# A decoder block on one core: squares read from the copied row, attention's low weight parts made by GpSimd, and the first gates' loads issued by GpSimd

## The chip, the core and the metric

The kernel runs on one core of a Trainium2 chip. The time is the device time of one execution in microseconds. The core has a matrix engine (PE), a vector engine (VectorE, DVE), an activation engine (ScalarE, ACT), GpSimd (POOL) and SyncE (SP), which issues most of the transfers. Each engine works through a queue of its own in order; between the queues, semaphores hold an instruction back until what it needs is done.

## What is computed

One layer over x of 1024 tokens by 1024 channels, in float32. Cut to what matters here:

```python
h = rms_norm(x, attn_norm_w)
q, k, v, u, g = split(h @ w_in)            # 1024 x 7168
q = rms_norm(q per head half); k = rms_norm(k per head half)
p = softmax(q1 k1^T * scale + bias, causal) - lam * softmax(q2 k2^T * scale + bias, causal)
y_a = (rms_norm(p @ v per head) * (1 - lam_init)) @ w_proj_attn
c = silu(layer_norm(causal_depthwise_conv(u_a * sigmoid(u_b), width 31)))
y_b = c @ w_proj_conv
x = x + (sigmoid(g_a) * y_a + sigmoid(g_b) * y_b) @ w_out
h = rms_norm(x); x = x + (silu(h @ W_gate) * (h @ W_up)) @ w_down
```

There are 8 heads; q and k are split into two halves of 64, v is 128 wide.

## The kernel before

Every product of float32 numbers is made of three matrix products: each operand is split in a high part, which ACT makes by a cast (`split_hi`, L120), and a low part, the original less the high part (`split_lo` on DVE, L125). L168, L169 and L170 are the three products. The weights pass through this split too: `wraw` is loaded, `whi` cast, `wlo` subtracted. Which engine subtracts a weight's low part is decided by a switch, `low_by_pool`: while it is set, `low` uses POOL (L131), otherwise DVE.

The stages follow one another in time roughly so:

- 0 to 248 us: normalized x, then the columns of V and u and the first conv tiles, with the switch set.
- 248 to 300 us: Q item 0 and the last of V.
- 300 to 822 us: attention. PE does heads 0 to 7 (scores `sc`, transposes `pT` of the weights, products `pW` with v), and fills the gaps with Q items 1 to 7 (`q_item`: a head's q and k columns, one `whi`/`wlo` pair for each half) and G items 0 to 15 (`g_item`: gate columns, one pair each, stored to `g_d`). On DVE the taps of the depthwise convolution (L594) run in between, one multiply-add for each of 31 taps, the first by ACT. The accumulator `acc` of a conv tile lies in PSUM for tiles 0 to 3 and in SBUF for tiles 4 to 7 (`CONV_PSUM` is 4).
- 822 to about 1000 us: the output projection of the heads (`aT`), gates for it, and the conv branch's layer norm and projection.
- After that w_out and the channel mixer, to 1726 us.

In attention L1291 adds the bias table `tb` to the scores in PSUM and takes the running maximum (E), L1296 on ACT exponentiates, L1306 forms the difference of the two softmax halves in `E` (SBUF), L1328 transposes it on PE.

A Q item works on banks `pg` of 512 columns in PSUM. For each bank ACT copies the bank to an SBUF row `raw` (tile name `qkraw`, L797) and makes eight squares of 64 columns with a running sum (L800, tile name `jk`), both from the bank; DVE then scales the row by the root (L807) and PE transposes it (L815). The rows are then split, and parts of them are copied between partitions by SP's transfers (L826 to L837), since two halves of 64 share 128 partitions. The first scores of the next head wait for those copies.

Heads 0 to 4 of the attention output are read back early from memory: five loads `early` (L1492) into attention's buffers `E`, of which there are four, each followed by a cast to `aTh` (ACT) and a low part `aTl` (DVE). Then follow `part`, a memset on POOL, the loads of heads 5 and 6, and `ln_step`, which begins the layer norm's chain for the mean: on SP a load of the conv tiles' sum and eight loads of `cT_lo`, then PE's `mean`. After it the first four gates are loaded by SP (`gated`, L1632) from `g_d`, and ACT takes their sigmoid (L1633); DVE multiplies them into the projection's banks (L1640).

The order of each engine's queue is not written out by hand: a scheduler lays the instructions out by the costs that it holds for them and by what depends on what, so that a moved piece of work moves others. What the program does fix are the conditions `after(...)`, by which a piece isn't issued before another.

Of the kernel before, what the change touches and what calls it, by code (L numbers as in the profile page):

```python
# [10 lines left out]
F32 = mybir.dt.float32  # L11
F32R = mybir.dt.float32r
AF = mybir.ActivationFunctionType
# [3 lines left out]
P = 128  # L17
# [3 lines left out]
HD = 64  # L21
VD = 128
# [35 lines left out]
def kernel(  # L58
# [27 lines left out]
    nc = tc.nc  # L86
    dve, act, pool, pe = nc.vector, nc.scalar, nc.gpsimd, nc.tensor
# [11 lines left out]
    sm = ctx.enter_context(tc.tile_pool(name="sm", bufs=4))  # L99
# [12 lines left out]
    def nm(s):  # L112
        uid[0] += 1
        return f"{s}_{uid[0]}"

    def f32(ap):
        return ap.bitcast(F32)
# [9 lines left out]
    low_by_pool = [False]  # L127
# [7 lines left out]
    def after(ins):  # L135

        return nullcontext() if ins is None else tc.issue_after(ins)

    def last_of(engine):
        for ins in reversed(nc.cur_bb.bb.instructions):  # L140
            if ins.engine == engine:
                return ins
# [11 lines left out]
    def pg():  # L154
        npg[0] += 1
        p_, tag = pgs[npg[0] % len(pgs)]
        return p_.tile([P, 512], F32, tag=tag, name=nm("pg"))
# [4 lines left out]
    def pm(z="pm"):  # L162
        npm[0] += 1
        p_, tag = pms[npm[0] % len(pms)]
        return p_.tile([P, 512], F32, tag=tag, name=nm(z))
# [86 lines left out]
    def pcol(key, k=0):  # L252
        c = col[key] + k
        return pvec[:, c : c + 1]
# [89 lines left out]
    class Stream:  # L344
# [12 lines left out]
        def next(self):  # L357
            self.fetch()
            return self.have.pop(0)
# [6 lines left out]
    def gemm_T(w, mhi, mlo, sb, amid=None):  # L366

        o = pg()
        cs = slice(sb * 512, (sb + 1) * 512)
        for k in range(NKT):  # L370
            mm3(o[:], w[0][:, k, :], w[1][:, k, :], kt(mhi, k)[:, cs], kt(mlo, k)[:, cs], k == 0, k == NKT - 1)
            if amid is not None and k == NKT // 2 - 1:
                amid()
        return o

    def gemm_N(o, halves, shi, slo, i):

        ts = slice(i * P, (i + 1) * P)
        for k in range(NKT):
            whi, wlo = halves[k // 4]  # L380
            mm3(o, kt(shi, k)[:, ts], kt(slo, k)[:, ts], whi[:, k % 4, :], wlo[:, k % 4, :], k == 0, k == NKT - 1)
# [8 lines left out]
    g_d = [dr.tile([P, S], F32, name=f"g_d{c}") for c in range(2 * NKT)]  # L390
# [289 lines left out]
    def rstd_of(ss, n, scale, fast=False):  # L680
        v = sm.tile([P, 16], F32, tag="v", name=nm("v"))[:, :n]
        dve.tensor_scalar(v, ss, scale, EPS, op0=ALU.mult, op1=ALU.add)
        return rsq(v, n, fast)
# [99 lines left out]
    T = {}  # L783
    late = []

    def q_item(h):
        halves = [ws.next(), ws.next()]
        t = {}
        T[h] = t
        for b in (1, 0):  # L790
            raw = qkp.tile([P, 4, 256], F32, tag="qkraw", name=nm("qkraw"), bufs=2)
            ss = sm.tile([P, 16], F32, tag="ss16", name=nm("ss16"))
            for i2 in range(2):
                o = pg()
                for e in range(2):
                    gemm_N(o[:, 256 * e : 256 * (e + 1)], halves, hT_hi, hT_lo, 4 * b + 2 * i2 + e)
                act.copy(raw[:, 2 * i2 : 2 * i2 + 2, :], o[:].rearrange("p (e c) -> p e c", c=256))  # L797
                jk = sm.tile([P, VD], F32, tag="jk", name=nm("jk"), bufs=1)[:, :HD]
                for g in range(8):
                    act.activation(  # L800
                        jk, o[:, g * HD : (g + 1) * HD], AF.Square, accum_out=ss[:, 8 * i2 + g : 8 * i2 + g + 1]
                    )
                if i2 == 0:
                    yield
            r = rstd_of(ss[:], 16, 1.0 / HD, fast=h > 0)
            r4 = raw[:].rearrange("p i (g d) -> p (i g) d", d=HD)
            dve.tensor_tensor(r4, r4, r.unsqueeze(2).to_broadcast([P, 16, HD]), op=ALU.mult)  # L807

            def turn_qk(z, key, b, raw):


                dma = nc.sync.dma_start
                pt = pm("pQ")
                for i in range(4):
                    pe.transpose(pt[:, i * P : (i + 1) * P], raw[:, i, z * P : (z + 1) * P], ident[:])  # L815
                w = pcol(key + "n")

                def part(j):
                    return qkp.tile([P, 512], F32R, tag=f"{key}s{j}", name=f"{key}s{j}_{h}_{b}", bufs=2 if key == "q" else 3)

                s1, s2 = part(1), part(2)
                act.activation(s1[:], pt[:], AF.Identity, scale=w)
                lo = part(3) if key == "q" else qkp.tile([P, 512], F32R, tag="klo", name=f"klo_{h}_{b}", bufs=1)
                dve.scalar_tensor_tensor(lo[:], pt[:], w, f32(s1[:]), op0=ALU.mult, op1=ALU.subtract)
                if key == "q":
                    dma(f32(s2[HD:, :]), f32(s1[HD:, :]))  # L826
                    lo2 = part(4)
                    for one, two in ((s1, s2), (lo, lo2)):
                        if one is lo:
                            dma(f32(two[HD:, :]), f32(one[HD:, :]))  # L830
                        dma(f32(two[:HD, :]), f32(one[HD:, :]))
                        dma(f32(one[HD:, :]), f32(one[:HD, :]))
                    t["q", b] = (s1, lo), (s2, lo2)
                else:
                    act.activation(s2[HD:, :], pt[HD:, :], AF.Identity, scale=w[HD:, :])
                    dma(f32(s2[:HD, :]), f32(lo[HD:, :]))
                    dma(f32(s1[HD:, :]), f32(lo[:HD, :]))  # L837
                    t["k", b] = s1, s2

            for z, key in ((1, "k"), (0, "q")):
                free = NT * (h - 1) + (0 if key == "k" and b else NT if key == "q" and not b else NT // 2)
                late.append((free if h else 0, lambda a_=(z, key, b, raw): turn_qk(*a_)))
            yield

    inatt = [False]
    MAKE = {"V": v_item, "U": u_item, "Q": q_item, "G": g_item}

    def run(items):  # L850
# [394 lines left out]
        due -= int(due)  # L1245
    while late:
        late.pop(0)[1]()
    low_by_pool[0] = False
    pcv_ctx.close()
    pgs.pop()  # L1250
    pg2_ctx.close()
# [264 lines left out]
    with after(m):  # L1516
        for _ in fill:
            pass
    inatt[0] = False
    del pms[1:]  # L1520
    at_ctx.close()

# [9 lines left out]
    for h in (5, 6):  # L1532
        for sb in range(2):
            cs = slice(sb * 512, (sb + 1) * 512)
# [79 lines left out]
    def ln_step():  # L1614
        for _ in range(lnp.pop(0)):
            next(lnq, None)
# [8 lines left out]
    lp = ln_ctx.enter_context(tc.tile_pool(name="lnp", bufs=2, reuse_waits="tile"))  # L1625
    gts, ngt = [(bp, "gt")], [0]

    def gated(d, cs):
        ngt[0] += 1
        p_, tag = gts[ngt[0] % len(gts)]  # L1630
        g = p_.tile([P, 512], F32, tag=tag, name=nm("gt"), bufs=4)
        nc.sync.dma_start(g[:], d[:, cs])  # L1632
        act.activation(g[:], g[:], AF.Sigmoid)  # L1633
        return g

    def ya_out(c, os2, gs=None):
        for sb in range(2):
            cs = slice(sb * 512, (sb + 1) * 512)
            g = gs[sb] if gs else gated(g_d[c], cs)
            dve.tensor_tensor(g[:], os2[sb][:], g[:], op=ALU.mult)  # L1640
            nc.sync.dma_start(ya_d[c][:, cs], g[:])

    ln_step()
    mean_hi = last_of(mybir.EngineType.Activation)

    NE = 2
    with after(last_of(mybir.EngineType.Activation)):
        g3 = [[gated(g_d[c], slice(sb * 512, (sb + 1) * 512)) for sb in range(2)] for c in range(NE)]
    first_gates = last_of(mybir.EngineType.Activation)
    w3 = [ws.next()]  # L1650
    with after(mean_hi), after(first_gates):
        w3.append(ws.next())
    o3 = [[pg() for sb in range(2)] for c in range(NE)]
    for k in range(NKT):
        for c in range(NE):
            for sb in range(2):
                cs = slice(sb * 512, (sb + 1) * 512)
                with after(last_mean[0]):
                    mm3(o3[c][sb][:], w3[c][0][:, k, :], w3[c][1][:, k, :], aT_hi[k][:, cs], aT_lo[k][:, cs], k == 0, k == NKT - 1)
        if k == NKT - 2:  # L1660
            with after(last_mm[0]):
                ln_step()
    for c in range(NE):
        ya_out(c, o3[c], g3[c])
    with after(first_gates):
        ln_step()
    for c in range(NE, NKT):
        with after(mean_hi if c == NE else None), after(first_gates if c == NE else None):
            w = ws.next()
# [11 lines left out]
    for cl in ((0, 1, 2), (3, 4), (5, 6), (7,)):  # L1681
        pair = [(c, ws.next()) for c in cl]
        for sb in range(2):
            cs = slice(sb * 512, (sb + 1) * 512)
            for c, w in pair:
                g = gated(g_d[NKT + c], cs)
                ya = bp.tile([P, 512], F32, tag="ya", name=nm("ya"), bufs=4)
                nc.sync.dma_start(ya[:], ya_d[c][:, cs])
                o = gemm_T(w, cT_hi, cT_lo, sb)
# [102 lines left out]
    o = {}  # L1792
# [342 lines left out]
```

## Time and profile before

| | us |
|---|---|
| median of 3 runs (lowest to highest) | 1726.91 (1726.63 to 1727.03) |
| span of the profiled execution | 1725.7 |
| median less span | 1.2 |
| PE busy | 1714.6 |
| DVE busy | 1275.4 |
| ACT busy | 862.5 |
| POOL busy | 219.1 |

The span runs from the first instruction to the last of one execution. The median of the runs is 1.2 us longer than it. Busy time counts the work of each engine and not its waits. A row of a group of instructions gives the line, the engine, the operation, output<-inputs with the shapes, how often it occurred, busy time and mean duration in ns, and the idle time of the engine just before, with what ended it. The views of a tile give minimum, median and maximum in ns, and the start of the first and of the last.

### The profile page before, as it was taken

Reading aid. Unit: us, or ns where it says so; the run is one execution under the profiler, and the core shown is the slowest. Engines: PE = TensorE matmul, PEld = TensorE weight load, DVE = VectorE, ACT = ScalarE, POOL = GpSimd, SP = SyncE. Lnnn points to the kernel's source line nnn. Section 1 sums busy time; section 2 is a strip of 40 time slices with the busy share of each in tenths; the row PEclk is TensorE's granted clock in tenths of the full one; section 3 lists DMA queues with packets and bytes.
Section 4 is the critical chain, followed back from the end, with each engine's and each line's share of the span. In section 5 each row is a group of like instructions: output and inputs, shape, how many; then the busy total and the mean of one; then the engine's idle time right before and its main releaser. Section 6 shows DMA issues by size and latency. Waiting matters only on the chain.

```text
span 1725.7 us, 25863 instructions
## 1 busy us (share of the span) xinstructions
PE 1714.6 (99%) x9243; PEld 1477.9 (86%) x9243; DVE 1275.4 (74%) x2128; ACT 862.5 (50%) x1958; POOL 219.1 (13%) x207
## 2 busy tenths in 40 slices
PE   9999999999999999999999999999999999999999
PEld 7997889998998998988788888888888888888887
DVE  7675889898988888878687769966676666575544
ACT  5333335767777776756556325633333333333332
POOL 3997851000000000000000000000000000000000
PEclk9999999999999999999999999999999999999999
DMA  6344445336345344343973683245455445598663
GB/s 208 116 126 132 131 151 154 104 109 171 104 127 147 115 125 138 101 136 130 333 238 118 200 296 119 74 135 164 147 170 170 154 141 164 175 355 285 217 215 130
DMA packets 261604, 281.64 MB, mean 163 GB/s; under 512 B 16546, under 2 KB 181986, under 8 KB 261475
## 3 DMA queue, kind: packets, MB, share of 16 engines
q1 hardware_dynamic: 254160, 267.71, 48.3%
q0 software_dynamic: 5680, 9.39, 2.6%
q10 hardware_dynamic: 1634, 2.89, 0.5%
q8 instruction: 73, 1.20, 0.3%
q14 instruction: 57, 0.46, 0.1%
HBM read 181.84 MB, written 85.50 MB: 155 GB/s over the span
## 4 chain that ended last, share of the span: by engine, by line
PE 92%; DMA 3%; DVE 2%; ACT 1%; issue 1%; POOL 0%; SPq 0%; DVEq 0%; POOLq 0%; ACTq 0%
PE acc L980 29%; PE acc L488 12%; PE pg L168 12%; PE pg L169 12%; PE pg L170 12%; PE wo L1850 3%; PE sc L1290 2%; PE sc L1289 2%; PE pT L1328 2%; PE pg L1106 1%; DVE acc L594 1%; PE pW L168 1%; PE pW L169 1%; PE pW L170 1%; PE pQ L815 1%
## 5 line engine op out<-in xcount | busy, mean ns | idle before, releaser
L594 DVE SCALAR_TENSOR_TENSOR acc<-u,cw,acc 128x1023 f32<-128x1023 f32 (+14 forms) x240 | 303.4, 1264 | 23.2 <-ACT acc L588 20.7
L170 PE MATMUL pg<-whi,hT_lo 128*128 128x256 f32 x704 | 200.2, 285 | 0.0
L168 PE MATMUL pg<-whi,hT_hi 128*128 128x256 f32 x704 | 199.7, 285 | 0.4 <-DVE v L125 0.4
L169 PE MATMUL pg<-wlo,hT_hi 128*128 128x256 f32 x704 | 199.5, 284 | 0.0
L125 DVE TENSOR_TENSOR wlo<-draw,whi 128x1024 fp32r<-128x1024 f32 x75 | 91.7, 1223 | 83.4 <-ACT whi L120 78.9
L120 ACT CAST whi<-draw 128x1024 fp32r<-128x1024 f32 x75 | 79.1, 1055 | 129.5 <-PE acc L488 114.3
L169 PEld LDWEIGHTS pg<-wlo,hT_hi 128*128 128x128 f32 x704 | 134.4, 191 | 1.8
L170 PEld LDWEIGHTS pg<-whi,hT_lo 128*128 128x128 f32 x704 | 134.3, 191 | 1.8
L168 PEld LDWEIGHTS pg<-whi,hT_hi 128*128 128x128 f32 x704 | 134.0, 191 | 2.1 <-DVE v L125 0.6
L120 ACT CAST whi<-wraw 128x1024 fp32r<-128x1024 f32 x90 | 94.7, 1052 | 70.6 <-PE pg L169 32.6
L488 PE MATMUL acc<-wlo,whi 128*128 128x512 f32 x308 | 119.8, 389 | 0.0
L488 PE MATMUL acc<-whi,wlo 128*128 128x512 f32 x308 | 119.8, 389 | 0.0
L1296 ACT ACTIVATE E<-E,mn 128x640 f32<-128x640 f32 (+7 forms) x128 | 99.8, 781 | 30.8 <-DVE mn L1291 29.2
L168 PE MATMUL pg<-hT_hi,whi 128*128 128x512 f32 x288 | 114.4, 397 | 0.1
L169 PE MATMUL pg<-hT_lo,whi 128*128 128x512 f32 x288 | 113.7, 395 | 0.0
L170 PE MATMUL pg<-hT_hi,wlo 128*128 128x512 f32 x288 | 113.7, 395 | 0.0
L120 ACT CAST whi<-s 128x1024 fp32r<-128x1024 f32 x54 | 56.9, 1053 | 104.9 <-PE acc L980 101.8
L125 DVE TENSOR_TENSOR wlo<-wraw,whi 128x1024 fp32r<-128x1024 f32 x75 | 93.3, 1246 | 12.6 <-ACT whi L120 12.3
L1291 DVE CUSTOM_DVE_ANT_0 E<-sc,tb 128x512 f32<-128x512 f32 (+3 forms) x128 | 74.2, 585 | 33.2 <-PE pT L1328 16.1
L980 PE MATMUL acc<-h_hi,whi 128*128 128x512 f32 x240 | 93.4, 389 | 0.0
L980 PE MATMUL acc<-h_lo,whi 128*128 128x512 f32 x240 | 93.4, 389 | 0.0
L980 PE MATMUL acc<-h_hi,wlo 128*128 128x512 f32 x240 | 90.1, 389 | 0.0
(370 smaller groups left out, 4589.7 us busy)
## 6 DMA issues: line engine op xcount, KB each, us to landing
wraw<-in_w_gate_up_dram SPq DMA_DIRECT2D x44, 512.0 KB, 4.7
wraw<-in_w_in_dram SPq DMA_DIRECT2D x38, 512.0 KB, 4.0
qs<-qs SPq DMA_DIRECT2D x96, 128.0 KB, 2.3
wd<-in_w_down_dram SPq DMA_DIRECT2D x44, 256.0 KB, 3.1
tdT<-wd SPq DMA_DIRECT2D x88, 128.0 KB, 4.8
draw<-sdS SPq DMA_DIRECT2D x44, 256.0 KB, 3.7
draw<-tdT SPq DMA_DIRECT2D x44, 256.0 KB, 3.7
wraw<-in_w_in_dram SPq DMA_DIRECT2D x32, 256.0 KB, 3.3
```

Of the source, the lines that this page charges most:

```text
L120: act.copy(dst, src)
L125: last_lo[0] = dve.tensor_tensor(dst, src, f32(hi), op=ALU.subtract).ins
L168: pe.matmul(o, lh, rh, start=start, stop=False)
L169: pe.matmul(o, lh, rl, start=False, stop=False)
L170: last_mm[0] = pe.matmul(o, ll, rh, start=False, stop=stop).ins
L488: m = pe.matmul(o[s_][i][:], l_[:, ts], r_[:, 512:], start=start and j + y_ == 0, stop=j == n - 1 and y_ == 2, skip_group_check=not start,)
L594: dve.scalar_tensor_tensor(a_, us[c][:, : S - n], cw[:, c, t : t + 1], a_, op0=ALU.mult, op1=ALU.add)
L980: last_mm[0] = pe.matmul(o[:], a_[x_][:, k, :], b_[y_][:, k, :], start=start and k + x_ + y_ == 0, stop=k == 3 and x_ == 1, skip_group_che ...
L1289: pe.matmul(o[:, :w], qh[:, qs], k, start=True, stop=False)
L1291: dve.tensor_tensor_reduce(e[:, ks], o[:, :w], tb[:, S - nk + c0 : S - nk + c0 + w], 1.0, mn[:, j : j + 1] if c0 else 3.0e38, ALU.add, ALU ...
L1296: act.activation(e[:, :nk], e[:, :nk], AF.Exp, bias=mn[:, j : j + 1], scale=-1.0, accum_out=l[:, j : j + 1])
L1850: last_mm[0] = pe.matmul(o[s_][i][:], A[u_], B[v_], start=start and j + y_ == 0, stop=j == 3 and y_ == 2, skip_group_check=not start,).ins
```

## The change

Three pieces. First, in a Q item the squares are taken from the SBUF row `raw` instead of the bank `o`, by a new function `q_squares`. Second, the switch `low_by_pool` is cleared after attention rather than before it, so that the weights' low parts of the Q items 1 to 7 and the G items are made by POOL. Third, the first four gate loads are issued on POOL's queue, ahead of `ln_step`, and their sigmoids stand where the loads with their sigmoids stood.

```diff
--- before.py
+++ after.py
@@ -783,6 +783,14 @@
     T = {}
     late = []
 
+    def q_squares(raw, ss, tiles):
+        for i in tiles:
+            jk = sm.tile([P, VD], F32, tag="jk", name=nm("jk"), bufs=1)[:, :HD]
+            for g in range(4):
+                act.activation(
+                    jk, raw[:, i, g * HD : (g + 1) * HD], AF.Square, accum_out=ss[:, 4 * i + g : 4 * i + g + 1]
+                )
+
     def q_item(h):
         halves = [ws.next(), ws.next()]
         t = {}
@@ -795,11 +803,7 @@
                 for e in range(2):
                     gemm_N(o[:, 256 * e : 256 * (e + 1)], halves, hT_hi, hT_lo, 4 * b + 2 * i2 + e)
                 act.copy(raw[:, 2 * i2 : 2 * i2 + 2, :], o[:].rearrange("p (e c) -> p e c", c=256))
-                jk = sm.tile([P, VD], F32, tag="jk", name=nm("jk"), bufs=1)[:, :HD]
-                for g in range(8):
-                    act.activation(
-                        jk, o[:, g * HD : (g + 1) * HD], AF.Square, accum_out=ss[:, 8 * i2 + g : 8 * i2 + g + 1]
-                    )
+                q_squares(raw, ss, (2 * i2, 2 * i2 + 1))
                 if i2 == 0:
                     yield
             r = rstd_of(ss[:], 16, 1.0 / HD, fast=h > 0)
@@ -1245,7 +1249,6 @@
         due -= int(due)
     while late:
         late.pop(0)[1]()
-    low_by_pool[0] = False
     pcv_ctx.close()
     pgs.pop()
     pg2_ctx.close()
@@ -1517,6 +1520,7 @@
         for _ in fill:
             pass
     inatt[0] = False
+    low_by_pool[0] = False
     del pms[1:]
     at_ctx.close()
 
@@ -1625,11 +1629,15 @@
     lp = ln_ctx.enter_context(tc.tile_pool(name="lnp", bufs=2, reuse_waits="tile"))
     gts, ngt = [(bp, "gt")], [0]
 
-    def gated(d, cs):
+    def gate_load(d, cs, queue=nc.sync):
         ngt[0] += 1
         p_, tag = gts[ngt[0] % len(gts)]
         g = p_.tile([P, 512], F32, tag=tag, name=nm("gt"), bufs=4)
-        nc.sync.dma_start(g[:], d[:, cs])
+        queue.dma_start(g[:], d[:, cs])
+        return g
+
+    def gated(d, cs):
+        g = gate_load(d, cs)
         act.activation(g[:], g[:], AF.Sigmoid)
         return g
 
@@ -1640,12 +1648,15 @@
             dve.tensor_tensor(g[:], os2[sb][:], g[:], op=ALU.mult)
             nc.sync.dma_start(ya_d[c][:, cs], g[:])
 
+    NE = 2
+    g3 = [[gate_load(g_d[c], slice(sb * 512, (sb + 1) * 512), pool) for sb in range(2)] for c in range(NE)]
     ln_step()
     mean_hi = last_of(mybir.EngineType.Activation)
 
-    NE = 2
     with after(last_of(mybir.EngineType.Activation)):
-        g3 = [[gated(g_d[c], slice(sb * 512, (sb + 1) * 512)) for sb in range(2)] for c in range(NE)]
+        for gs in g3:
+            for g in gs:
+                act.activation(g[:], g[:], AF.Sigmoid)
     first_gates = last_of(mybir.EngineType.Activation)
     w3 = [ws.next()]
     with after(mean_hi), after(first_gates):
```

Line numbers of the kernel after are higher by 3 or 4 in attention and by 4 to 8 at the gates. The scheduler lays the queues out anew; the rows here are what stands in a queue, one after the other, before and after.

POOL's queue at the beginning of attention (`wlo` is a weight's low part, `cs_d` adds a conv tile to the sum in memory, `pl` and `ph` are attention's memsets). Before:

```order
L131 TENSOR_TENSOR wlo_2557<-wraw_2554,whi_2556 128x1024
L131 TENSOR_TENSOR wlo_2876<-wraw_2872,whi_2875 128x1024
L131 TENSOR_TENSOR wlo_2883<-wraw_2879,whi_2882 128x1024
L578 DMA cs_d<-c_d_140 512x256
L1319 MEMSET pl_3608 128x128
L1318 MEMSET ph_3607 128x128
L1319 MEMSET pl_3809 128x128
L1318 MEMSET ph_3808 128x128
L1319 MEMSET pl_3942 128x128
```

After:

```order
L131 TENSOR_TENSOR wlo_2557<-wraw_2554,whi_2556 128x1024
L131 TENSOR_TENSOR wlo_2880<-wraw_2876,whi_2879 128x1024
L131 TENSOR_TENSOR wlo_2887<-wraw_2883,whi_2886 128x1024
L131 TENSOR_TENSOR wlo_3194<-wraw_3191,whi_3193 128x1024
L578 DMA cs_d<-c_d_140 512x256
L131 TENSOR_TENSOR wlo_3200<-wraw_3197,whi_3199 128x1024
L131 TENSOR_TENSOR wlo_3656<-wraw_3652,whi_3655 128x1024
L1322 MEMSET pl_3616 128x128
L1321 MEMSET ph_3615 128x128
L131 TENSOR_TENSOR wlo_3849<-wraw_3845,whi_3848 128x1024
L131 TENSOR_TENSOR wlo_3994<-wraw_3991,whi_3993 128x1024
L1322 MEMSET pl_3817 128x128
```

Low parts now stand between the memsets and behind the transfer of `cs_d`: the fourth row of the piece after is the first of 30 that were not in this queue.

SP's queue where head 6's q and k rows are copied (`qs`, `ks`), around the store `g_d_155` of a gate, which waits for ACT's sgg, and the conv tile's store `c_d_143`. Before:

```order
L826 DMA qs_6_1_7992<-qs_6_1_7991 64x512
L831 DMA qs_6_1_7992<-qs_6_1_7991 64x512
L600 DMA c_d_143<-acc_6344 128x1024
L830 DMA qs_6_1_7997<-qs_6_1_7994 64x512
L832 DMA qs_6_1_7991<-qs_6_1_7991 64x512
L831 DMA qs_6_1_7997<-qs_6_1_7994 64x512
L869 DMA tb_8238<-t_d_319 128x1024
L640 DMA g_d_155<-sgg_8223 128x512
L832 DMA qs_6_1_7994<-qs_6_1_7994 64x512
```

After:

```order
L835 DMA qs_6_1_8020<-qs_6_1_8019 64x512
L834 DMA qs_6_1_8025<-qs_6_1_8022 64x512
L835 DMA qs_6_1_8025<-qs_6_1_8022 64x512
L836 DMA qs_6_1_8019<-qs_6_1_8019 64x512
L840 DMA ks_6_0_8037<-klo_0_8039 64x512
L836 DMA qs_6_1_8022<-qs_6_1_8022 64x512
L841 DMA ks_6_0_8036<-klo_0_8039 64x512
L600 DMA c_d_143<-acc_6364 128x1024
L640 DMA g_d_155<-sgg_8181 128x512
L873 DMA tb_8266<-t_d_319 128x1024
L640 DMA g_d_155<-sgg_8251 128x512
```

The last copy of this head's q rows stood behind the store of the gate and the table `tb`; now all of them stand ahead of the conv tile's store, the gate's stores and the table.

PE's last transposes of attention (`pT`). Before:

```order
L1328 MATMUL pT_9710<-ident,E_9608 128x128
L1328 MATMUL pT_9742<-ident,E_9690 128x128 x2
L1348 MATMUL pB_9803<-ident,ar_9686 128x128 x2
L168 MATMUL pW_9811<-ph_9706,vh_9162 128x256
L169 MATMUL pW_9811<-pl_9707,vh_9162 128x256
```

After:

```order
L1331 MATMUL pT_9742<-ident,E_9640 128x128
L1331 MATMUL pT_9774<-ident,E_9722 128x128 x2
L170 MATMUL pg_9807<-hT_hi,wlo_9502 128x512
L168 MATMUL pg_9807<-hT_hi,whi_9501 128x512
L169 MATMUL pg_9807<-hT_lo,whi_9501 128x512
```

The two transposes are rows 4643 and 4644 of PE's queue before and 4624 and 4625 after, 19 rows earlier; the output projection begins at row 4677 in both. It uses heads 0 to 3 for two banks and more, 48 matmuls, before head 4 in the kernel before; in the kernel after it uses head 4 after 12 matmuls.

DVE's low parts of the five early heads. In the kernel before `early_9765`, `9767`, `9820`, `9822` and `9828` are heads 0 to 4; in the kernel after `early_9797`, `9799`, `9852`, `9854` and `9860`. Before:

```order
L125 TENSOR_TENSOR pl_9707<-pT_9742,ph_9706 128x2x128
L125 TENSOR_TENSOR aTl_9759<-early_9765,aTh_9753 128x1024
L125 TENSOR_TENSOR aTl_9760<-early_9767,aTh_9754 128x1024
L125 TENSOR_TENSOR aTl_9761<-early_9820,aTh_9755 128x1024
L125 TENSOR_TENSOR aTl_9762<-early_9822,aTh_9756 128x1024
L125 TENSOR_TENSOR wlo_9969<-wraw_9966,whi_9968 128x1024
L682 TENSOR_SCALAR v_9844<-ssa_9517 128x8
L125 TENSOR_TENSOR aTl_9763<-early_9828,aTh_9757 128x1024
```

After:

```order
L125 TENSOR_TENSOR pl_9739<-pT_9774,ph_9738 128x2x128
L125 TENSOR_TENSOR aTl_9793<-early_9852,aTh_9787 128x1024
L125 TENSOR_TENSOR aTl_9794<-early_9854,aTh_9788 128x1024
L125 TENSOR_TENSOR aTl_9791<-early_9797,aTh_9785 128x1024
L125 TENSOR_TENSOR aTl_9792<-early_9799,aTh_9786 128x1024
L125 TENSOR_TENSOR aTl_9795<-early_9860,aTh_9789 128x1024
L125 TENSOR_TENSOR wlo_10001<-wraw_9998,whi_10000 128x1024
L682 TENSOR_SCALAR v_9876<-ssa_9549 128x8
```

Heads 2 and 3 now come first, then 0 and 1, then 4.

## Prediction

> **What bounds the kernel now.** I read the page first, then the windows, then PE's waits, because a part with no idle time can only be sped up by giving it less to do.
>
> ```profile
> span 1725.7 us, 25863 instructions
> PE 1714.6 (99%) x9243; PEld 1477.9 (86%) x9243; DVE 1275.4 (74%) x2128; ACT 862.5 (50%) x1958; POOL 219.1 (13%) x207
> PE 92%; DMA 3%; DVE 2%; ACT 1%; issue 1%; POOL 0%; SPq 0%; DVEq 0%; POOLq 0%; ACTq 0%
> ```
>
> PE is busy 99% of the span and is 92% of the chain that ended last. The change takes no matmul away, so it can only win PE's idle time. It touches the program from about 300 us (attention) to about 860 us (the first gates). The windows split that stretch; the columns are the window's length, then each engine's busy time.
>
> ```profile
> core 0: us, PE busy (x) PEld busy (x) DVE busy (x) ACT busy (x) POOL busy (x), PEclk, DMA share, GB/s
> 248.00:300.00 52.00, 51.64 (x421) 50.95 (x420) 47.10 (x54) 27.07 (x90) 12.69 (x9) 1.00 0.66 183
> 300.00:400.00 100.00, 100.00 (x688) 92.72 (x687) 89.47 (x184) 69.21 (x241) 3.08 (x10) 1.00 0.42 116
> 400.00:500.00 100.00, 99.88 (x699) 92.74 (x698) 84.09 (x195) 73.92 (x243) 3.73 (x14) 1.00 0.46 132
> 500.00:600.00 100.00, 98.92 (x684) 91.33 (x683) 87.38 (x204) 75.51 (x265) 4.75 (x17) 1.00 0.47 134
> 600.00:700.00 100.00, 99.16 (x692) 92.02 (x691) 85.42 (x187) 70.43 (x235) 4.14 (x16) 1.00 0.46 128
> 700.00:780.00 80.00, 80.00 (x478) 70.38 (x477) 65.11 (x149) 53.19 (x159) 1.45 (x8) 1.00 0.43 126
> 780.00:820.00 40.00, 39.53 (x228) 34.04 (x227) 31.80 (x69) 24.79 (x70) 2.34 (x8) 1.00 0.36 118
> 820.00:860.00 40.00, 38.98 (x174) 31.27 (x174) 23.20 (x34) 19.53 (x34) 0.00 (x0) 1.00 0.97 332
> ```
>
> Window length less PE's busy time gives PE's idle time: 0.36, 0, 0.12, 1.08, 0.84, 0, 0.47, 1.02, together 3.89 us. DVE is the fullest of the others: 411.5 us of the 480 from 300 to 780, 86%. POOL is nearly empty (17 of 480). The waits of PE between 245 and 845 us name the causes (total us, times, longest):
>
> ```profile
> PE sc L1289 <- DMA ks<-klo: 1.1, 1, 1.1
> PE sc L1290 <- DMA qs<-qs: 0.8, 1, 0.8
> PE pg L168 <- ACT sgg L639: 0.4, 1, 0.4
> PE pg L168 <- DVE v L125: 0.4, 1, 0.4
> PE pg L169 <- DVE aTl L125: 0.2, 1, 0.2
> ```
>
> The two longest are for transfers, not for an engine. Matmuls overlap, so an idle piece understates its loss. Round the qs wait (start, duration):
>
> ```profile
> 690.08 0.36 PE L168 MATMUL pg<-whi,hT_hi 128*128 128x256 f32 x1
> 690.28 0.28 PE L169 MATMUL pg<-wlo,hT_hi 128*128 128x256 f32 x1
> 691.40 0.50 PE L1290 MATMUL sc<-ks,qs 128*128 128x512 f32 x1 [0.84 <-DMA qs<-qs]
> ```
>
> Start to start this gap is 1.12 us, where the one before it is 0.20: about 0.9 to 1.0 is lost for 0.84 listed, and more in proportion where the gap is small. I scale the 3.89 us by 1.35 (an estimate) and take 5.3 us, 0.3%, as the most that can be won.
>
> **Part 1: squares from the copied row.** Of each bank ACT makes one copy and eight squares; now only the copy reads the bank.
>
> ```profile
> L797 ACT COPY qkraw<-pg x32: 564/587/612, 254.2 to 717.6; 128x512 f32<-128x512 f32 x32
> L800 ACT ACTIVATE jk<-pg x256: 200/224/269, 254.7 to 723.2; 128x64 f32<-128x64 f32 x128
> 399.69 0.68 ACT L639 ACTIVATE sgg<-pg,pvec 128x512 f32<-128x512 f32 x1
> ```
>
> Nothing is added or removed: 32 copies and 256 squares stay. A bank comes free after 0.59 us rather than after at least another 8 x 0.22 = 1.8 us. That matters only where PE waits for a bank: in the list of waits once, 0.4 us, behind the sgg at 399.69 that stands among squares. What hides the rest is that the other bank has work. Reading SBUF instead of PSUM is not in the trace for a square; 256 x 0.02 us either way would be 5 us on an engine that is 70% busy, and off the path. I take -0.5 us (range -0.5 to 0).
>
> **Part 2: 30 low parts move from DVE to POOL.** Two for each of seven Q items, one for each of 16 G items. Rows of DVE between 300 and 780 us, then POOL's low parts (min/median/max ns):
>
> ```profile
> L125 DVE TENSOR_TENSOR wlo<-wraw,whi 128x1024 fp32r<-128x1024 f32 x28 | 34.1, 1219 | 2.8 <-ACT whi L120 2.7
> L594 DVE SCALAR_TENSOR_TENSOR acc<-u,cw,acc 128x995 f32<-128x995 f32 (+14 forms) x113 | 142.5, 1261 | 2.9 <-ACT acc L588 2.8
> L1306 DVE SCALAR_TENSOR_TENSOR E<-E,rl,E 128x896 f32<-128x896 f32 (+7 forms) x58 | 48.0, 828 | 0.5
> L131 POOL TENSOR_TENSOR wlo<-wraw,whi x15: 2388/2409/2461, 74.5 to 296.2; 128x1024 fp32r<-128x1024 f32 x15
> ```
>
> DVE is relieved of 30 x 1.22 = 36.6 us; POOL takes on 30 x 2.41 = 72.3 us, which it has room for. But the trace shows what a POOL low part does to DVE. Both engines at 271 us, and the usual durations of the two DVE rows concerned:
>
> ```profile
> 271.60 1.95 DVE L657 TENSOR_TENSOR r<-r,t 128x16 f32<-128x16 f32 x1
> 273.47 1.26 DVE L594 SCALAR_TENSOR_TENSOR acc<-u,cw,acc 128x1009 f32<-128x1009 f32 x1
> 274.65 2.31 DVE L807 TENSOR_TENSOR qkraw<-qkraw,r 128x1024 f32<-128x1024 f32 x1
> 271.12 4.77 POOL L131 TENSOR_TENSOR wlo<-wraw,whi 128x1024 fp32r<-128x1024 f32 x2 [17.17 <-ACT whi L120]
> L657 DVE TENSOR_TENSOR r<-r,t 128x16 f32<-128x16 f32 (+1 forms) x20 | 3.4, 168 | 0.1
> L807 DVE TENSOR_TENSOR qkraw<-qkraw,r x16: 1207/1218/2311, 274.6 to 729.3; 128x1024 f32<-128x1024 f32 x16
> ```
>
> The two-input operation L657 lasted 1.95 us instead of 0.17 and ended when POOL's first low part did (271.12 + 2.41 = 273.5); L807 took 2.31 instead of 1.22. The tap between them, whose accumulator is in PSUM there (tile 3), lost nothing. So a low part on POOL cost DVE 1.78 and 1.09 us, mean 1.44, when an operation with both inputs in SBUF came up. In attention the taps (tiles 4 to 7) accumulate in SBUF, as L1306 and L807 do: 142.5 + 48.0 + 17 us, over half of the 377 that DVE keeps. The cost lies between 0 and 30 x 1.44 = 43 us; I take three quarters, 32 us, against the 36.6 saved, so DVE's load stays as it is.
>
> The Trainium skill says this too (SBUF — State Buffer, "Who interferes with whom"): a DVE instruction with two SBUF inputs contends with a GpSimd instruction that reads SBUF, and whoever issues first holds the shared ports for its whole instruction. By that rule the change would not relieve DVE as the low parts' durations alone promise; the rows at 271.60 and 274.65 us agree.
>
> What matters is PE. The blocks fall where the order of DVE did not plan them. The one place where the trace shows two, 271 to 277 us, is followed by one PE wait for DVE (v L125, 0.4 us): at most 0.2 per block, 30 x 0.2 = 6 us; at least 0, if DVE's 14% of idle time swallows all. Nearest to attention, where PE never waited for DVE from 300 to 780, is the low end: I take 30 x 0.05 = +1.5 us. POOL's own queue adds a wait: low parts stand behind memsets that wait for PE.
>
> ```profile
> L1319 POOL MEMSET pl<- 128x128 f32 x29 | 6.0, 206 | 404.3 <-PE pW L169 312.8 <-PE pW L170 38.1 <-DVE rl L1304 20.5
> ```
>
> PE itself releases those, and a weight is cast up to a buffer's turn ahead of its use; I put this at 0, and at one 2.41 us piece if it misses once.
>
> **The order that comes of it: head 6.** With other costs the queues are laid out anew. SP now sends head 6's q copies ahead of the gate stores, which wait for sgg on ACT; before, the last of them stood behind one. So the qs wait goes: -1.0 us (range -1.0 to 0). The ks wait of 1.1 I leave.
>
> **The order that comes of it: heads 0 to 4.** Before, head 4's rows are needed after 48 matmuls of the output projection, now after 12.
>
> ```profile
> L125 DVE TENSOR_TENSOR aTl<-early,aTh x5: 1224/1225/1226, 818.4 to 827.6; 128x1024 fp32r<-128x1024 f32 x5
> DMA to landing us min/median/max: 3.5/6.1/7.3
> 821.30 1.05 ACT L120 CAST aTh<-early 128x1024 fp32r<-128x1024 f32 x1 [0.88 <-DMA early<-a_d]
> L168 PE MATMUL pg<-aTh,whi x18: 388/389/497, 822.6 to 835.3; 128*128 128x512 f32 x18
> ```
>
> PE begins at 822.6; the 18 triples to 835.3 start 0.75 us apart (12.7 / 17), so four triples later, at 825.6, it now wants head 4. Head 4's load waits for a buffer that the first low part of the five frees; from that (818.4 + 1.2 = 819.6) to head 4's low part ready (827.6 + 1.2 = 828.8) were 9.2 us, most of it the load. Now the first of the five is head 2. Its cast stood at 821.30; the transposes that free its buffer stand 19 PE rows earlier, at most 19 x 0.25 = 4.7 us: cast at 816.6, low part ready 1.05 + 1.22 later at 818.9, head 4 ready at 828.1, a stall of 2.5. With the shortest landing (3.5 instead of 6.1) there is none. I take 2.0, less the 0.4 (0.2 listed) that PE loses here before: +1.6 us (range -0.4 to +3).
>
> **Part 3: first gate loads by POOL.**
>
> ```profile
> L1632 SPq DMA_DIRECT2D gt<-g_d x4: 319/320/320, 836.9 to 838.9; - x4
> L1633 ACT ACTIVATE gt<-gt x4: 630/632/633, 842.1 to 844.0; 128x512 f32<-128x512 f32 x4
> ```
>
> Four loads of 256 KB leave SP's queue at 836.9 and are read at 842.1; on POOL they stand behind the memset of part, past no waiting work. No PE wait there is for them, so the gain is 0. Moving 1.05 MB ahead of other loads at 332 GB/s costs those 3.2 us at worst; I take 0, as the loads' casts have other work before them.
>
> **Sum.** The profiled span is 1725.7, the median 1726.9, so 1.2 us lie outside. -0.5 + 1.5 - 1.0 + 1.6 = +1.6: 1727.3 + 1.2 = 1728.5 us.
>
> **Rivals.**
> - Slower: the blocks reach PE. Mechanism: POOL holds DVE in front of L1306 and the pieces that PE's transposes wait for. At 0.2 per block +6 instead of +1.5 gives 1733.0. For it: DVE 86% full, blocks of up to 1.78. Against: no PE wait for DVE from 300 to 780. It decides from about 0.11 us per block, which is 1730.3. Chance 0.28.
> - Faster: taps with an SBUF accumulator are not blocked (no row shows one beside a POOL low part), DVE is 36.6 us lighter, and the waits listed shrink. All 5.3 us give 1721.6; with the head 4 stall left, about 1723. Chance 0.18.
> - The change doesn't do what it says: banks, loads and DVE were not what PE waited for, and the reordering cancels: 1726.9. Chance 0.14, within the same verdict.
> - Forecast: 0.40.
>
> **How the numbers follow.** A difference under 0.2% (3.5 us) can't be told from none in this kernel. Forecast and third rival are within it, 0.54. The range 1722.8 to 1733.6 leaves out the fastest half of the second rival and the part of the first in which more than 0.2 us per block reaches PE.
>
> **What would show it.** Right: POOL busy about 72 us more; DVE taps or L1306 of 1.8 to 3 us beside POOL's low parts; no qs wait; a PE wait for aTl of 1 to 3 us near 825; no wait for sgg at 400. Wrong: DVE's busy time down by 30 us or more with no long taps, or PE waiting for E, pl or sc many times, or for gt.

## The result: 1734.9 us, slower by half a per cent

| | before | after |
|---|---|---|
| median of 5 runs (lowest to highest), us | 1726.87 (1725.71 to 1727.03) | 1734.89 (1734.42 to 1734.98) |
| span of the profiled execution | 1725.7 | 1732.9 |

The ratio is 1.0046, with a 95% interval of 1.0035 to 1.0057. The time lies 1.3 us above the predicted range; the rival that the prediction priced at 1733.0 is what happened.

The page of the kernel after, the engines' busy time:

```profile
span 1732.9 us, 25852 instructions
PE 1715.7 (99%) x9243; PEld 1476.9 (85%) x9243; DVE 1285.4 (74%) x2098; ACT 871.5 (50%) x1958; POOL 297.1 (17%) x241
```

POOL took on 78 us. DVE handed over 30 low parts and is busy 10 us more; the time for which an operation is held up counts as busy here, as the rows below show. The windows of the kernel before and then of the kernel after, in the three stretches that the change touches (length, PE busy, PEld, DVE, ACT, POOL):

```profile
300.00:780.00 480.00, 477.96 (x3232) 439.19 (x3232) 411.48 (x912) 342.26 (x1141) 17.15 (x65) 1.00 0.45 127
780.00:860.00 80.00, 78.52 (x401) 65.31 (x400) 55.00 (x103) 44.32 (x103) 2.34 (x8) 1.00 0.66 225
860.00:1000.00 140.00, 140.00 (x631) 116.11 (x630) 106.39 (x182) 73.03 (x115) 0.58 (x1) 1.00 0.56 185
```

```profile
300.00:780.00 480.00, 472.31 (x3196) 431.71 (x3194) 418.57 (x876) 346.36 (x1136) 85.38 (x92) 1.00 0.44 125
780.00:860.00 80.00, 80.00 (x414) 67.74 (x413) 55.39 (x104) 45.18 (x104) 11.63 (x15) 1.00 0.65 219
860.00:1000.00 140.00, 139.07 (x625) 115.03 (x624) 104.72 (x181) 74.18 (x116) 0.54 (x1) 1.00 0.58 192
```

PE's idle time went from 2.0 to 7.7 us in attention, from 1.5 to 0 round the end of attention, and from 0 to 0.9 behind it. Most of the loss is in the first row (5.7 us), and there PE waits for DVE, which it had not done before at all. PE's waits between 300 and 780 us, after:

```profile
PE sc L1292 <- DVE mn L1294: 3.3, 5, 0.9
PE sc L1292 <- DMA ks<-klo: 1.6, 2, 1.4
PE pT L1331 <- DVE qs L828: 1.1, 1, 1.1
PE pT L1331 <- DVE E L1309: 0.7, 1, 0.7
PE pQ L819 <- DVE qkraw L811: 0.4, 1, 0.4
PE pW L168 <- DVE pl L125: 0.3, 1, 0.3
PE pS L1372 <- DVE pl L125: 0.3, 1, 0.3
```

One of them followed back. The timelines of DVE, POOL and PE, after:

```profile
327.32 2.17 DVE L657 TENSOR_TENSOR r<-r,t 128x16 f32<-128x16 f32 x1
329.42 3.22 DVE L1309 SCALAR_TENSOR_TENSOR E<-E,rl,E 128x768 f32<-128x768 f32 x1
326.79 5.03 POOL L131 TENSOR_TENSOR wlo<-wraw,whi 128x1024 fp32r<-128x1024 f32 x2 [13.96 <-ACT whi L120]
332.69 0.55 PE L1331 MATMUL pT<-ident,E 128*128 128x128 f32 x3 [0.71 <-DVE E L1309]
```

POOL makes a Q item's two low parts from 326.79 to 331.82. DVE's L657, usually 0.17 us, ends when the first is done, and L1309, usually 1.02 us on this shape, ends 0.8 us after the second; the transpose of E on PE waits 0.71 us for it. Not every wait of the list is like this: the first of the mn waits, 0.84 us at 314.21, has no lengthened operation ahead of it but a tap of the usual 1.28 us. The groups of DVE in attention show which operations suffer. Before (busy us, mean ns), then after:

```profile
L1306 DVE SCALAR_TENSOR_TENSOR E<-E,rl,E 128x896 f32<-128x896 f32 (+7 forms) x58 | 48.0, 828 | 0.5
L1304 DVE SCALAR_TENSOR_TENSOR rl<-rl,neglam,l 128x1 f32<-128x1 f32 x58 | 12.4, 214 | 0.5
L654 DVE TENSOR_TENSOR t<-r 128x16 f32<-128x16 f32 (+1 forms) x20 | 3.3, 165 | 0.5 <-ACT r L650 0.5
```

```profile
L594 DVE SCALAR_TENSOR_TENSOR acc<-u,cw,acc 128x995 f32<-128x995 f32 (+14 forms) x111 | 145.2, 1308 | 7.3 <-ACT acc L588 7.3
L1309 DVE SCALAR_TENSOR_TENSOR E<-E,rl,E 128x896 f32<-128x896 f32 (+7 forms) x58 | 63.0, 1086 | 0.7
L1307 DVE SCALAR_TENSOR_TENSOR rl<-rl,neglam,l 128x1 f32<-128x1 f32 x58 | 19.0, 328 | 0.7
L654 DVE TENSOR_TENSOR t<-r 128x16 f32<-128x16 f32 (+1 forms) x20 | 10.9, 544 | 2.2 <-ACT r L650 2.2
L1294 DVE CUSTOM_DVE_ANT_0 E<-sc,tb 128x512 f32<-128x512 f32 (+3 forms) x118 | 68.4, 589 | 20.9 <-PE sc L1293 7.6 <-DMA tb<-t_d 6.4 <-PE pT L1331 5.0
```

L1309 grew by 15.0 us, L1307 by 6.6, L654 by 7.6, the taps by 5.2 (111 x 0.047). L1294, which takes one input from PSUM, kept its mean (589 ns, 591 before). Counted operation by operation, 24 operations between 300 and 820 us lasted over 0.25 us longer than the median of their line and shape, by 40.9 us together; before there was none.

### The profile page after: what moved, and what is told of

Read it like the earlier page. It is cut to its first block, busy times and chain, and to the rows that moved or that the text cites. A ratio compares the mean times of both kernels' runs of the same rounds, so it can differ in the third digit from the quotient of the medians.

```text
span 1732.9 us, 25852 instructions
## 1 busy us (share of the span) xinstructions
PE 1715.7 (99%) x9243; PEld 1476.9 (85%) x9243; DVE 1285.4 (74%) x2098; ACT 871.5 (50%) x1958; POOL 297.1 (17%) x241
## 4 chain that ended last, share of the span: by engine, by line
PE 85%; DVE 9%; ACT 3%; DMA 2%; issue 1%; SPq 0%; DVEq 0%; ACTq 0%
PE acc L984 30%; PE acc L488 12%; PE pg L168 10%; PE pg L170 10%; PE pg L169 10%; DVE acc L594 3%; PE wo L1861 3%; PE sc L1292 1%; PE sc L1293 1%; PE pT L1331 1%; PE pg L1110 1%; DVE E L1294 1%; DVE E L1309 1%; PE pW L168 1%; PE pW L170 1%
## 5 line engine op out<-in xcount | busy, mean ns | idle before, releaser
L594 DVE SCALAR_TENSOR_TENSOR acc<-u,cw,acc 128x1023 f32<-128x1023 f32 (+14 forms) x240 | 310.5, 1294 | 27.0 <-ACT acc L588 24.5
L131 POOL TENSOR_TENSOR wlo<-wraw,whi 128x1024 fp32r<-128x1024 f32 x45 | 112.8, 2511 | 272.3 <-ACT whi L120 257.4
L1294 DVE CUSTOM_DVE_ANT_0 E<-sc,tb 128x512 f32<-128x512 f32 (+3 forms) x128 | 73.5, 584 | 21.0 <-PE sc L1293 7.6
```

What stands on the lines that cost most here:

```text
L131: pool.tensor_tensor(dst, src, f32(hi), op=ALU.subtract)
L594: dve.scalar_tensor_tensor(a_, us[c][:, : S - n], cw[:, c, t : t + 1], a_, op0=ALU.mult, op1=ALU.add)
L1294: dve.tensor_tensor_reduce(e[:, ks], o[:, :w], tb[:, S - nk + c0 : S - nk + c0 + w], 1.0, mn[:, j : j + 1] if c0 else 3.0e38, ALU.add, ALU ...
```

## Experiments

Medians, ratios to the kernel before in the same runs with 95% intervals, lengthened operations (counted as above) and PE's idle time in attention (480 us less its busy time in the window 300 to 780):

| run | median us | ratio (95%) | lengthened, sum us | PE idle us |
|---|---|---|---|---|
| squares alone | 1725.49 | 0.9991 (0.9982 to 1.0000) | 0 | 0.9 |
| low parts alone | 1740.16 | 1.0073 (1.0060 to 1.0086) | 25, 45.4 | 9.5 |
| all without low parts | 1730.38 | 1.0023 (1.0014 to 1.0032) | 0 | 0.1 |
| all, quarters | 1729.53 | 1.0021 (1.0010 to 1.0033) | 45, 21.6 | 1.8 |
| squares, quarters | 1725.16 | 0.9995 (0.9986 to 1.0004) | 46, 21.8 | 1.6 |
| squares, eighths | 1723.78 | 0.9983 (0.9974 to 0.9992) | 18, 4.9 | 0.0 |
| squares, whole low parts | 1733.86 | 1.0038 (1.0026 to 1.0051) | 24, 41.3 | 7.1 |
| gates alone | 1731.37 | 1.0026 (1.0017 to 1.0035) | 0 | 0.6 |
| gates, by SP | 1731.38 | 1.0039 (1.0025 to 1.0052) | 0 | 1.3 |
| all, eighths | 1727.84 | 1.0013 (1.0005 to 1.0022) | 16, 4.3 | 0.0 |

### The parts one by one

Squares alone: the kernel before with `q_squares`.

```diff
                 act.copy(raw[:, 2 * i2 : 2 * i2 + 2, :], o[:].rearrange("p (e c) -> p e c", c=256))
-                jk = sm.tile([P, VD], F32, tag="jk", name=nm("jk"), bufs=1)[:, :HD]
-                for g in range(8):
-                    act.activation(
-                        jk, o[:, g * HD : (g + 1) * HD], AF.Square, accum_out=ss[:, 8 * i2 + g : 8 * i2 + g + 1]
-                    )
+                q_squares(raw, ss, (2 * i2, 2 * i2 + 1))
```

> The kernel before with only part 1 (squares from the copied row); gates and low parts as before. Theory of the blocks (POOL's low parts hold DVE in two-input operations, and that is where the 8 us come from): this kernel has no such blocks in attention, so it lies within 1.5 us of before, 1725.5 to 1728.5, with no DVE operation above its usual duration after 300 us. Rival, squares: ACT's squares now wait for the copy and shift the order so that PE waits for DVE or ACT; then this kernel alone shows a good part of the loss, 1730 or more.

Measured 1725.49: no loss, and at most a small gain, since the interval ends at 1.0000. PE's waits between 245 and 845 us, squares alone:

```profile
PE sc L1293 <- DVE mn L1295: 0.9, 2, 0.5
PE pg L168 <- DVE v L125: 0.8, 1, 0.8
PE pg L168 <- ACT sgg L639: 0.4, 1, 0.4
```

The wait for the bank behind sgg, the one that part 1 was priced by, is still there; the two waits for transfers (1.1 and 0.8) are not. So the small gain isn't the bank's earlier release; the order is new too, and it probably comes from that, which isn't shown.

Low parts alone: the kernel before with the switch cleared later.

```diff
-    low_by_pool[0] = False
     pcv_ctx.close()
...
     inatt[0] = False
+    low_by_pool[0] = False
```

> The kernel before with only part 2 (attention's low parts on POOL). Theory of the blocks: nearly the whole loss is here, 1732 to 1737, with about 24 lengthened DVE operations between 300 and 820 us that sum to about 40 us, as in the changed kernel. Rival, order: if the loss is an accident of one queue order, this other order gives 1727 or less although the blocks are there.

Measured 1740.16, over the expected range and the slowest of all: the blocks are there, and PE idles 9.5 us in attention and 2.1 between 780 and 860. The rival of an accident of one order falls: this order, the changed kernel's and that of squares with whole low parts (below) all lose 7 to 10 us of PE's time in attention. But they don't lose alike. This one is 13.3 us slower than the kernel before, the other two 8.0 and 7.2. The 2.1 us between 780 and 860, most of it at 830 to 835 where PE waits for `aTl` and `aTh`, are a part of what it loses beyond them, and behind that wait the trace grants PE less than its full clock (1.00), 0.66 on average from 835 to 840 us, which is worth about 1.7 us more (0.34 x 5, an estimate). The rest is open.

All without low parts: the changed kernel with the switch cleared ahead of attention, as before.

```diff
+    low_by_pool[0] = False
     pcv_ctx.close()
...
     inatt[0] = False
-    low_by_pool[0] = False
```

> The changed kernel without part 2 (squares from the row and gate loads on POOL stay, low parts on DVE again). Theory of the blocks: 1724 to 1728, no lengthened DVE operation after 300 us; the 8 us are gone. Rival, squares or gates: at least half of the loss stays, 1731 or more.

Measured 1730.38, neither the one nor the other. The theory holds in attention, where no operation is lengthened and PE idles 0.1 us. But 3.5 us stay, from a place that no step had named: PE idles 4.0 us between 860 and 1000 us, round 940. There too the granted clock falls behind the wait (window, PE, PEld, DVE, ACT, POOL, clock):

```profile
945.00:950.00 5.00, 4.04 (x11) 3.21 (x12) 5.00 (x8) 1.69 (x4) 0.00 (x0) 0.66 0.80 241
```

### How long one piece is

Quarters: each low part in attention in four instructions of 256 columns.

```diff
-            pool.tensor_tensor(dst, src, f32(hi), op=ALU.subtract)
+            w = dst.shape[-1] // pieces[0]
+            for i in range(0, dst.shape[-1], w):
+                pool.tensor_tensor(dst[:, i : i + w], src[:, i : i + w], f32(hi)[:, i : i + w], op=ALU.subtract)
...
+    pieces[0] = 4
     pcv_ctx.close()
```

> The changed kernel with each low part that POOL makes in attention cut in four pieces of 256 columns, about 0.6 to 0.7 us each. Theory of the blocks, with the ports held for one whole instruction: a DVE operation now waits for one piece, at most about 0.7 us, so that the lengthened operations' sum falls from 41 us to 10 to 25 and the time to 1727 to 1731. Rival, lateness: if PE's loss comes from the low parts being late or from DVE's order, four pieces with their fixed costs are no earlier, and the time stays at 1734 or rises.

Measured 1729.53, as the theory of the blocks has it: the sum of the lengthened operations halves, none is more than 0.95 us over its median (2.52 in the changed kernel), and PE's idle time in attention falls from 7.7 to 1.8 us.

The next three leave part 3 out: squares with quarters, with eighths (`pieces[0] = 8`) and with whole low parts (`pieces[0] = 1`).

> Squares from the row and low parts on POOL in four pieces, but the gate loads as before (on SP, behind the layer norm's loads). In the run with quarters and in the one without low parts PE lost 5 to 7 us at 937 to 946 us, in the conv branch's projection, which the run with squares alone did not. Theory: that loss belongs to part 3 (with it the scheduler lays the projection out so that PE meets the layer norm's casts too early), so here it is gone: 1722 to 1726. Rival: it comes from the lighter DVE in attention or from chance in any new order; then it shows here as well: 1728 or more.

> Like the run with squares and quarters, but eight pieces of 128 columns. Theory of the blocks: a DVE operation waits for one piece at most, about 0.35 us; lengthened operations sum to about 10 us (whole 41, quarters 22), time equal to the quarters' within 1 us or up to 2 lower. Rival: what the quarters won was only another order; then the sum of the lengthened operations doesn't follow the piece's length, or the time doesn't follow that sum.

> Squares from the row and whole low parts on POOL, gate loads as before: the changed kernel without part 3. Theory of the blocks: it keeps the whole loss of attention, so 1732 to 1736, and is 7 to 11 us slower than the run with quarters beside it, from which it differs in the pieces alone. Rival: if part 3 made a good part of the changed kernel's loss, it is 1729 or less.

Measured 1725.16, 1723.78 and 1733.86: whole, quarters, eighths cost in order, and whole against quarters is 8.7 us in the same runs. The windows 300 to 780 of whole, quarters and eighths:

```profile
300.00:780.00 480.00, 472.89 (x3199) 432.25 (x3198) 420.42 (x879) 346.64 (x1137) 85.56 (x92) 1.00 0.44 125
```

```profile
300.00:780.00 480.00, 478.39 (x3245) 439.96 (x3244) 413.75 (x900) 353.75 (x1154) 118.11 (x176) 1.00 0.45 127
```

```profile
300.00:780.00 480.00, 480.00 (x3267) 442.40 (x3266) 406.96 (x907) 356.35 (x1158) 145.98 (x290) 1.00 0.45 127
```

Down the three rows POOL's busy time rises from 86 to 146 us, DVE's falls from 420 to 407, and PE's idle time from 7.1 to 0. So it is not how much POOL works that hurts, but how long one of its instructions keeps DVE waiting. The limit of 0.25 us hides short delays of the eighths: counted from 0.1 us on, the lengthened operations of the three are 24, 52 and 53 and sum to 41.3, 23.0 and 10.6 us. The three orders aren't equal (of PE's 9243 matmuls some 1030 with quarters and 1090 with eighths differ from the one at that place with whole low parts), so a part of the difference may be the order's; that PE's idle time in attention also follows the pieces with part 3 in (7.7, 1.8 and 0 us) speaks against a large part. Squares with eighths beats both kernels: 0.9983 of the kernel before. Whether it beats the squares alone (0.9991) isn't shown, as the two intervals overlap.

### The gates

Gates alone: the kernel before with part 3; then the same with `nc.sync` as the loads' queue.

```diff
+    g3 = [[gate_load(g_d[c], slice(sb * 512, (sb + 1) * 512), pool) for sb in range(2)] for c in range(NE)]
     ln_step()
```

> The kernel before with only part 3 (first gate loads on POOL's queue). Theory: the loss of 5 to 7 us near 940 us belongs to part 3 alone: 1729 to 1733, with PE waiting for casts of cT and a weight there. Rival: it needs another part beside it (the order is an accident of the sum of changes): within 1.5 us of before, 1725.5 to 1728.5, no such waits.

> The kernel before with part 3, but the four gate loads stay on SP's queue, ahead of the layer norm's loads. Theory: what costs time in part 3 is not POOL's queue but that the loads are issued ahead of the mean's chain, after which the scheduler places the second half of the layer norm's rstd behind the first matmuls of the conv branch's projection (it does so in this kernel's order too): 1729 to 1733 with PE's waits for cT_hi and a weight near 940 us. Rival, POOL's queue: loads issued by POOL are the cause, so on SP the loss is gone: 1725.5 to 1728.

Measured 1731.37 and 1731.38: part 3 costs by itself 0.26% and 0.39%, and POOL's queue isn't the reason. PE's waits between 860 and 1000 us, gates alone:

```profile
PE pg L168 <- ACT cT_hi L120: 2.0, 2, 1.6
PE pg L168 <- ACT whi L120: 1.4, 1, 1.4
PE pg L170 <- DVE wlo L125: 1.2, 1, 1.2
```

There were none before. Idle time there is 4.8 and 3.2 us, 4.0 and 3.8 in all without low parts and all with quarters, less than the 5 to 7 that were expected. In the profiled execution of the gates alone the clock is 0.84 and 0.82 from 945 to 955 us, in that of the gates by SP it is 1.00 throughout, so that the lower clock isn't a fixed part of the loss. The layer norm's first step on DVE for the 16 half tiles, before and with the gates alone (min/median/max ns, start of the first and of the last):

```profile
L1592 DVE TENSOR_TENSOR lnz<-cT_lo,rstd x16: 678/680/687, 881.7 to 936.3; 128x512 f32<-128x512 f32 x16
```

```profile
L1592 DVE TENSOR_TENSOR lnz<-cT_lo,rstd x16: 676/680/689, 879.8 to 938.0; 128x512 f32<-128x512 f32 x16
```

The chain begins 1.9 us earlier and ends 1.7 us later, and PE, which reaches the conv branch's projection 3.2 us earlier (913.0 rather than 916.2), meets it. In the orders of these two kernels, of all without low parts, and of both runs of all parts with pieces, the second half's `rstd` stands behind the first four matmuls of that projection; in the other seven, before and the changed kernel among them, it stands ahead of them, and those idle 0 to 0.9 us there. In the five the last cast of `cT_hi` ends 26.5 to 28.7 us after the projection's first matmul, in the seven 22.7 to 23.9. So the place of the `rstd` goes along with the loss in all twelve orders; that it is the cause isn't shown, and what in part 3 makes the scheduler place it so is open.

All, eighths: the changed kernel with `pieces[0] = 8`.

> The whole changed kernel with eight pieces for each low part in attention, so the run with squares and eighths plus part 3. Theory: the two losses add; attention keeps what the eighths gained and part 3 costs its 4 to 7 us near 940: 1727.5 to 1731. Rival: part 3 pays once DVE is relieved: 1724 or less.

Measured 1727.84: the parts add, 0.9983 without part 3 and 1.0013 with it. Attention has no PE idle time, and PE idles 3.2 us between 860 and 1000. With whole low parts they don't add: there the `rstd` stands ahead, and part 3 comes to 1.0 us.

## Why the prediction was wrong, step by step

**The bound was the right one.** PE's idle time over the whole span rose from 11.1 to 17.2 us (span less PE busy), 5.1 of that between 300 and 1000 us (windows above), and its busy time by 1.1 with the same matmuls; together that is the 7.2 us of the span. The prediction's own sign of being wrong came: in the list after, PE waits for E once, for pl twice, and before its scores five times for DVE's mn.

**Part 2, the blocks: the mechanism was right, the load nearly so.** Forecast were 32 us of lengthening against 36.6 saved, "DVE's load stays as it is". Measured were 40.9 (24 operations, 1.7 each, nearer to the bound of 43) and a DVE that is 7 us busier in attention.

**What reaches PE: the step that failed.** "I take 30 x 0.05 = +1.5 us", with 0.2 a block as the most. The experiments give 8.7 us for whole low parts against quarters: 0.36 for each of the 24 blocks, near seven times the step and above its upper bound. Against the kernel before, which still has the 30 low parts on DVE, part 2 costs 7.2 us with the squares and 13.3 alone. The bound came from one stretch before attention, and the low end from the absence of PE waits for DVE in attention. That absence showed that DVE, undisturbed, was in time; it didn't show by how much. In the stretch followed back, the two low parts of a Q item made DVE late twice in a row, by 2.0 and 2.2 us, and PE waited 0.71: the margin there was about 3.5 us (an estimate from these three), enough for one block and not for two. The blocked L1309 stands in the chain from scores to transposes, and PE's queue is in order.

**Part 1: -0.5 forecast, -1.4 measured alone** (0.9991, interval up to 1.0000), by another way than named: the bank's wait stayed in that run. A square takes longer from the row than from the bank, a median of 257 ns against 224; ACT's 256 squares are some 8 us longer, off PE's path.

**Head 6: right.** The qs wait is gone from the list after; ks waits of 1.6 stay.

**Heads 0 to 4: wrong in sign.** Forecast +1.6 us; PE's idle time from 780 to 860 went from 1.5 to 0. The rows after for the loads, head 4's cast and DVE's low part of it, and PE's first product:

```profile
DMA to landing us min/median/max: 3.7/4.1/4.8
830.32 1.05 ACT L120 CAST aTh<-early 128x1024 fp32r<-128x1024 f32 x1 [0.81 <-DMA early<-a_d]
831.40 1.23 DVE L125 TENSOR_TENSOR aTl<-early,aTh 128x1024 fp32r<-128x1024 f32 x1 [0.81 <-ACT aTh L120]
830.16 0.48 PE L168 MATMUL pg<-aTh,whi 128*128 128x512 f32 x1
```

PE wanted head 4 about 3 us after 830.16, and it was ready at 832.6. The order was read rightly; the loads landed in 4.1 us, not 6.1. I had taken one moment's median for a property of the load. Why they were quicker isn't shown: the DMA engines were as full, 0.98 and 1.11 from 815 to 825 us before, 0.98 and 1.16 from 820 to 830 after.

**Part 3: 0 forecast, +1.0 here** (1734.89 against 1733.86 without it, with overlapping intervals of the ratios) and +4.7 alone. The step looked at the loads and at who waits for them, and not at what the scheduler makes of the layer norm behind them.

**The sum.** In place of -0.5 + 1.5 - 1.0 + 1.6 stands, by runs: squares and whole low parts +7.2 (1733.86 against 1726.65), part 3 +1.0. The prediction held that less than 0.2% can't be told from none; with intervals of about 0.1% either way, the experiments told 0.17% (squares with eighths).

The Trainium skill's rule (SBUF — State Buffer, "Who interferes with whom") is borne out further than the prediction used it. It says that a DVE instruction outside the two-port modes with one SBUF input isn't blocked, but that `tensor_scalar` can enter those modes. L1294 agrees with the first (589 ns, 591 before). For the second, DVE and POOL in the run of the low parts alone:

```profile
403.72 2.35 DVE L682 TENSOR_SCALAR v<-ssa 128x8 f32<-128x8 f32 x1 [0.86 <-ACT jk L1356]
403.27 2.76 POOL L131 TENSOR_TENSOR wlo<-wraw,whi 128x1024 fp32r<-128x1024 f32 x1
```

A TENSOR_SCALAR with one input, usually 0.17 us, ended when POOL did.

## What to carry to other kernels

Work handed from DVE to POOL is free only where DVE's next instructions aren't among those that POOL's hold up, as 24 were here; price it by how long one POOL instruction lasts and by who waits for the DVE operation behind it, not by the busy time that DVE loses. Where it must be POOL, cut its instructions: eight pieces cost POOL nearly twice the time and gave back the whole loss of attention. And an engine on which the bound engine never waits may still have no slack: absence of waits is no measure of margin.

## What the hardware showed beside that

The blocking goes both ways. POOL's low parts in attention, whole (changed kernel), in quarters and in eighths (squares with quarters, squares with eighths; min/median/max ns, start of the first and of the last):

```profile
L131 POOL TENSOR_TENSOR wlo<-wraw,whi x30: 2381/2406/3390, 299.5 to 817.6; 128x1024 fp32r<-128x1024 f32 x30
```

```profile
L134 POOL TENSOR_TENSOR wlo<-wraw,whi x119: 716/741/1789, 299.9 to 811.0; 128x256 fp32r<-128x256 f32 x119
```

```profile
L134 POOL TENSOR_TENSOR wlo<-wraw,whi x239: 445/463/1470, 299.8 to 809.3; 128x128 fp32r<-128x128 f32 x120
```

The medians give a piece's own price: 2.41, 0.74 and 0.46 us, which is about 0.19 us for each instruction and 2.17 ns for each column (worked out from the first two; the third then comes to 0.46). So four quarters take 2.96 us undisturbed and eight eighths 3.70. The means are higher, 2.56, 0.97 and 0.63 us, because some pieces are held up. The quarters that last 1.7 us and more end some 0.6 us after a DVE operation that was running when they began, mostly a tap or the difference of the softmax halves; the eighths of 1.4 us end some 0.3 us after one. So POOL's busy time, 76.7, 108.4 and 138.8 us, grows for two reasons: the fixed part of more instructions, and waits for DVE.
